# Three score windows and one turn window cut from one six-bank PSUM tile, in the attention of a hybrid transformer block

## Chip, cores and metric

The kernel runs on one core of a Trainium2 chip, in one launch. The metric is device time in microseconds (us). Several executions of a kernel are timed; one more is taken with the hardware profiler, and all rows shown here are from that one.

## The reference, cut to what matters

One layer: a conditioned RMSNorm of 512 latent tokens (and 256 context tokens) of width 2048, one input projection, then two branches. Branch A is attention with 12 query heads on 4 groups of keys and values, over 512 + 256 = 768 keys. Branch B is a Fourier mixing of 512 channels. Both are gated, projected, merged with sigmoid gates and projected once more, and a final RMSNorm follows. All in float32.

```python
q = _rope(_rmsnorm(_heads(p, OFF_Q, N_Q_HEADS), q_norm_g[l]), cos, sin) * q_scale
s = jnp.einsum('bqhgd,bkhd->bhgqk', qi, k, preferred_element_type=jnp.float32)
w = jax.nn.softmax(s, axis=-1).astype(v.dtype)
o = jnp.einsum('bhgqk,bkhd->bqhgd', w, v)
y_a = (attn * jax.nn.silu(z_a)) @ w_pa
y_b = (_fourier_mix(u_b) * jax.nn.silu(z_b)) @ w_pb
return (g_a * y_a + g_b * y_b) @ w_o
```

## The kernel before

Products in float32 are made of three matmuls (`mm3`, lines 294 to 298): each operand is split into a high and a low half (`split_from`, lines 161 to 163: ACT copies the high half, DVE subtracts it and so makes the low half), and high x high, high x low and low x high are added up in PSUM. The kernel is written in a framework that finds out itself which instruction must wait for which, orders each engine's instructions with a scheduler, and writes the waits into the program. So the order on an engine need not be that of the source.

The work has these stages:
- normalisation and the first columns of the input projection, and branch B's Fourier mixing (lines 408 to 658);
- eight groups of the input projection (lines 1028 to 1067), each with seven products of a fast matrix scheme (`Group.run`, line 734);
- the attention, a loop of 48 steps (lines 1185 to 1218), one for each head and 128 queries;
- the projection of branch A with the merge (lines 1278 to 1326);
- two output groups with the final norm (lines 1472 to 1489).

**PSUM** has eight banks of 512 float32 columns. From line 668 to the end one pool `psp` holds it. `pair` (line 695) gives a tile of two banks: the tag x has two buffers that take turns, and the tags y0 and y1 have one each, which alternate too.

A step of the attention takes these parts:
- `scores` (line 1115) takes the next x tile and writes 768 columns of it in six matmuls, 512 and 256 columns wide. DVE finds the negative maximum (line 1124), ACT the exponential with its sum (line 1126; a small second instruction reads the sum).
- `turn` (line 1138) transposes the probabilities of the step before, six transposes into the tile that holds the other of the y tags (`turned_y`, lines 1076 and 1140), and `split_from` makes their high and low halves, `pth` and `ptl`. `divide` takes the reciprocal of the sum and scales the gate.
- `values` (line 1149), once for two steps, multiplies the turned probabilities with the values: 18 matmuls of 256 columns and two transposes.
- `turn_queries` (line 1021) turns the queries of the next head, once for four steps.
- `filler` (line 1082) is work of branch B's projection, cut in 64 pieces of three matmuls, put between the parts of a step; `fill` asks for the next pieces. After every four pieces a copy (line 1102) takes the sum out.

`both` (line 1077) is one y tile for the whole attention: the first bank, `fill_acc`, is the fillings' accumulator, the second, `b1`, that of `values` and of the query turns. `get_keys` (line 1012) turns the keys of a group in an x tile; group 0's come before the attention, those of groups 1 to 3 in it.

In the last step the first two products of branch A's projection begin (`products`, line 1173; `first_sums`, line 1214). From there on `pair` serves the accumulators (line 1287), the turned merge (`turn_merged`, line 1235) and the output groups. In the very last product `Banks` (line 712) holds the sums as two x tiles, and `finish` (line 792) does the 24 matmuls of the first 128 tokens, calls `last` (line 1425), whose lines 1433 to 1437 read these sums, and then does the other 24.

Loads go over the queues of SP (weights, keys, values: `start_load`, line 183) and POOL (heads, line 1010).

Of the kernel before, what the change touches and what calls it, by code (L numbers as in the profile page):

```python
# [10 lines left out]
F32 = mybir.dt.float32  # L11
# [4 lines left out]
PSUM = bass.MemoryType.PSUM  # L16
DRAM = bass.MemoryType.DRAM

P = 128
# [8 lines left out]
NKEY = T + C  # L28
# [79 lines left out]
def block_kernel(ctx, tc, xT, ctx_rows, ctx_toks, x, c_row, w_ss, w_gate, vecs, qkg, rope, dft_c, dft_s,  # L108
# [4 lines left out]
    def region(name, side="left", **kw):  # L113
        st = ExitStack()
        return st, st.enter_context(tc.tile_pool(name=name, bufs=1, side=side, **kw))
# [22 lines left out]
    def uid(s):  # L138
        cnt[0] += 1
        return f"{s}{cnt[0]}"  # L140
# [20 lines left out]
    def split_from(src, hi, lo):  # L161
        nc.scalar.activation(hi, src, ACT.Copy)  # L162
        return nc.vector.tensor_tensor(lo, src, hi.bitcast(F32), op=ALU.subtract)  # L163
# [94 lines left out]
    def get(key):  # L258
        load_more()
        turn = [e for e in ahead if not e.aside]  # L260
        assert turn[0].key == key, (turn[0].key, key)
        for e in turn[: min(look[0], len(hl_pools))]:
            split_piece(e)
        load_more()
        e = turn[0]
        ahead.remove(e)
        free.extend(p[0::2] for p, _ in e.raws if p in retired)
        return e.raws[0][1] if e.kind == "raw" else e.out
# [15 lines left out]
    def take(shape, dt=F32, pool=None):  # L284
        p = next((p for p in free if p[0] is pool), free[0])
        free.remove(p)
        t = slot_tile(p, shape, dt)
        home[id(t)] = p, t
        return t

    def give(*ts):
        free.extend(home.pop(id(t))[0] for t in ts)

    def mm3(o, ah, al, bh, bl, start, stop, cont=False):

        nc.tensor.matmul(o, ah, bh, start=start, stop=False, skip_group_check=cont)  # L296
        nc.tensor.matmul(o, ah, bl, start=False, stop=False, skip_group_check=cont)  # L297
        nc.tensor.matmul(o, al, bh, start=False, stop=stop, skip_group_check=cont)  # L298
# [34 lines left out]
    def tiles(key):  # L333

        new = [take((1024,), F32R) for _ in range(2)]
        kept.setdefault(key, []).extend(new)
        return new
# [15 lines left out]
    flat = lambda v: v.rearrange("p t c -> p (t c)")  # L353
# [14 lines left out]
    for g in range(LAST + 1):  # L368
        for name in ONE_GROUP:
            if (g, name) == (LAST, "Q4"):  # L370
                stream_keys(0)
            if g == KV:
                f = CTX_FORMS.index(next(f for n, f, _, _ in PRODUCTS if n == name))
# [291 lines left out]
    evs, evp = region("evp", "right", reuse_waits="tile")  # L665
    new_ev = lambda: evp.tile([P, 2, 512], F32, tag="ev", bufs=4, name=uid("ev"))
    qzs, qzp = region("qzp", "right", reuse_waits="tile")
    psp = ctx.enter_context(tc.tile_pool(name="psp", bufs=1, space=PSUM, reuse_waits="tile"))
    last_y = [0]
    rows4 = lambda hi, lo: [(hi[:, j, :], lo[:, j, :]) for j in range(4)]  # L670

    def make_form(f, h):
# [20 lines left out]
        return rows4(hi, lo)  # L693

    def pair(tag, skip=0):
        if tag == "y":
            last_y[0] += 1 + skip
            return psp.tile([P, 2, 512], F32, tag=f"y{last_y[0] % 2}", bufs=1, name=uid(tag))
        return psp.tile([P, 2, 512], F32, tag=tag, bufs=2, name=uid(tag))
# [12 lines left out]
    class Banks:  # L712


        def __init__(self):
            self.b = [pair("x") for _ in range(2)]
# [4 lines left out]
    class Group:  # L721
# [12 lines left out]
        def run(self, name):  # L734
            form, which = next((f, c) for n, f, _, c in PRODUCTS if n == name)
            start = which not in self.acc
            if start:

                self.acc[which] = Banks() if self.last and which == "c" else pair(self.tags[which])
# [137 lines left out]
    class Context:  # L877
# [13 lines left out]
        def products(self, name, which, pc, w, start):  # L891
            a = self.acc[:, 1 if which == "b" else 0, :]
            for k in range(2):
                j = 2 * pc + k
                fh, fl = (f.parts[j // 4][:, j % 4 // 2, P * (j % 2) : P * (j % 2) + P] for f in self.f)
                mm3(a, fh, fl, w[0][:, k, :], w[1][:, k, :], start and pc == 0 and k == 0, pc == 3 and k == 1,
                    cont=not start)
# [23 lines left out]
        def values(self, b, v):  # L921
            nc.scalar.dma_start(by_group(v_d[:, :, 4 + b, :]), v.rearrange("p (g d) -> p g d", g=4))
# [60 lines left out]
    def load_row(half):  # L983
        row = crow[half] = take((1024,)) if half else rp.tile([P, 1024], F32, tag="raw1", bufs=1, name=uid("crow"))
        nc.gpsimd.dma_start(row, c_row[:, 1024 * half : 1024 * half + 1024].broadcast_to([P, 1024]))

    def silu_of_row(half):

        e, row = take((1024,)), crow[half]
        nc.scalar.activation(e, row, ACT.Tanh, scale=0.5)  # L990
        nc.vector.scalar_tensor_tensor(row, e, 1.0, row, op0=ALU.add, op1=ALU.mult)
        give(e)
# [15 lines left out]
    def load_head(h):  # L1008
        qz[h] = take((2, 4, HD))
        nc.gpsimd.dma_start(qz[h], qz_d[h])  # L1010

    def get_keys(g):
        raw = get(("K", g))
        tk = flat(pair("x"))
        for t in range(KT):
            nc.tensor.transpose(tk[:, t * P : (t + 1) * P], raw[:, t * P : (t + 1) * P], ident)
        keys = tiles(g)
        split_from(tk[:, :NKEY], *(w[:, :NKEY] for w in keys))
        kv[g] = tuple(keys) + get(("V", g))

    def turn_queries(h, tq):
        for t in range(4):
            nc.tensor.transpose(tq[:, t * P : (t + 1) * P], qz[h][:, 0, t, :], ident)
        qs[h] = take((2, T), F32R)
        split_from(tq, qs[h][:, 0, :], qs[h][:, 1, :])
# [47 lines left out]
    free += [(hm, f"s{(9 + i) % KK}") for i in range(KK)]  # L1073
    ats_, atp = region("atp", "right", reuse_waits="tile")

    turned_y = last_y[0] % 2
    both = pair("y")
    fill_acc, b1 = both[:, 0, :], lambda: both[:, 1, :]
    assert not any(p[0] is gvp or p[2] == "raw1" for e in ahead for p, _ in e.raws)
    ybs, S = {}, {}  # L1080

# [26 lines left out]
    def fill(n):  # L1108
        for _ in range(n):
            next(fl, None)  # L1110
# [4 lines left out]
    def scores(i):  # L1115
        h, t = divmod(i, 4)
        kh, kl = kv[h // GQ][:2]
        s = slice(t * P, (t + 1) * P)
        qh, ql = qs[h][:, 0, s], qs[h][:, 1, s]
        sc = flat(pair("x"))  # L1120
        for a, b in ((0, 512), (512, 768)):
            mm3(sc[:, a:b], qh, ql, kh[:, a:b], kl[:, a:b], True, True)
        mx = stats[:, 4 * (i % 4) : 4 * (i % 4) + 4]
        nc.vector.tensor_reduce(mx[:, 0:1], sc[:, :NKEY], axis=AX.X, op=ALU.max, negate=True)
        probs[i] = take((NKEY,))
        nc.scalar.activation(probs[i], sc[:, :NKEY], ACT.Exp, bias=mx[:, 0:1], accum_out=mx[:, 1:2])  # L1126
        if t == 3:
            give(qs.pop(h))

    def divide(i):  # L1130

        h, t = divmod(i, 4)
        z = qz[h][:, 1, t, :]
        r = stats[:, 4 * (i % 4) + 2 : 4 * (i % 4) + 3]
        nc.vector.reciprocal(r, stats[:, 4 * (i % 4) + 1 : 4 * (i % 4) + 2])
        nc.vector.tensor_scalar(z, z, r, None, op0=ALU.mult)

    def turn(i):
        p = probs.pop(i)
        tp = flat(psp.tile([P, 2, 512], F32, tag=f"y{turned_y}", bufs=1, name=uid("tp")))  # L1140
        for k in range(KT):
            nc.tensor.transpose(tp[:, k * P : (k + 1) * P], p[:, k * P : (k + 1) * P], ident)
        if i % 2 == 0:
            pts[i // 2] = [atp.tile([P, KT, 256], F32R, tag=n, bufs=2, name=uid(n)) for n in ("pth", "ptl")]
        c = slice((i % 2) * P, (i % 2) * P + P)
        split_from(tp[:, :NKEY].rearrange("p (k q) -> p k q", k=KT), *(w[:, :, c] for w in pts[i // 2]))
        give(p)
# [34 lines left out]
                        pc == 0 and k == 0, pc == BRANCH_A[-1] and k == 1)  # L1182
                yield pc, t

    filled = 0
    for i in range(NSTEP + 3):
        h, t = divmod(i, 4)
        if i < NSTEP:
            if t == 1 and h + 2 < NH:
                load_head(h + 2)  # L1190
            if i == 24:
                load_row(0)
            elif i == 28:
                silu_of_row(0)
            if i % 12 == 10 and i // 12 + 1 < NKV:
                get_keys(i // 12 + 1)
            scores(i)
        want = min(3 + 61 * (i + 1) // NSTEP, 64)
        if want > filled:
            fill(1)  # L1200
            filled += 1
        if i % 2 == 0 and i >= 4:
            values((i - 4) // 2)
        if 1 <= i <= NSTEP:
            turn(i - 1)
            divide(i - 1)
        if t == 1 and h + 1 < NH:
            turn_queries(h + 1, b1())
        if want > filled:
            fill(want - filled)  # L1210
            filled = want
        if i == NSTEP - 1:
            fill(1)
            first_sums = [pair("x") for _ in range(2)]
            first = products(CHUNKS[0], first_sums)
        if NSTEP > i - 2 >= NSTEP - 3:
            next(first)
            next(first)
# [12 lines left out]
    m = -1  # L1231
# [46 lines left out]
    for n, j in enumerate(CHUNKS):  # L1278
# [9 lines left out]
        for pc, t in products(j, accs) if n else first:  # L1288
# [4 lines left out]
            if pc > 3:  # L1293
                y = ybs[j, pc - 4]
# [274 lines left out]
```

## Time and profile before

| | us |
|---|---|
| median of 3 runs | 1335.85 |
| lowest and highest | 1332.83 and 1336.69 |
| the profiled execution | 1333.12 |
| its span, first to last instruction | 1331.3 |
| TensorE (PE) busy in it | 1298.5 |
| DVE, ACT and POOL busy | 977.9, 653.2 and 137.1 |
| the attention, first scores to last turn | 824.5 to 1027.3 |

A row of a group reads: line, engine, operation, what is written and read, shapes and count; then the busy time and the mean of one in nanoseconds; then the idle time of the engine just ahead of these instructions and who ended it. A row of a timeline reads: start, duration, engine, line, operation, and in brackets idle time ahead of it. A row of the waits reads: who waited for whom, us in total, how often, and the longest.

### The profile page before, as it was taken

How to read it: one execution, taken by the hardware profiler on the slowest of the kernel's cores; microseconds unless marked ns; L12 is line 12 of the kernel's file. 1: busy time of each engine (PE TensorE's matmuls, PEld its weight loads, DVE VectorE, ACT ScalarE, POOL GpSimd, SP SyncE). 2: the span in 40 equal slices, each digit the busy share in tenths (PEclk: the TensorE clock that was granted, in tenths of full speed). 3: DMA queues.
4: the chain of work that ended last, by engine and by line, in shares of the span. 5: the costliest groups of instructions: out<-in, count | busy, mean ns of one | idle time of the engine just before them, and what ended most of it. 6: DMA issues, size and time to landing. Idle time of an engine off the chain costs nothing. (4 is left out here: it accounts for less than half of the span.)

```text
span 1331.3 us, 17479 instructions
## 1 busy us (share of the span) xinstructions
PE 1298.5 (98%) x6594; PEld 1061.9 (80%) x6594; DVE 977.9 (73%) x1286; ACT 653.2 (49%) x1017; POOL 137.1 (10%) x186
## 2 busy tenths in 40 slices
PE   6999999999999999999999999999999999999996
PEld 3566888888888887888887888788888888887885
DVE  4655989887778867646477666677776789777677
ACT  5322655555555544544264455666665133364444
POOL 1110011210302011011021110000000100111210
PEclk9999999999999999999999999999999999999999
DMA  9996677887897999777669886122113899678983
GB/s 380 402 387 243 227 190 197 228 230 223 195 317 189 304 268 267 255 166 182 190 181 308 217 240 227 31 71 80 43 53 112 328 329 333 181 172 224 224 216 142
DMA packets 96085, 291.28 MB, mean 219 GB/s; under 512 B 8960, under 2 KB 32000, under 8 KB 91648
## 3 DMA queue, kind: packets, MB, share of 16 engines
q1 hardware_dynamic: 51600, 172.95, 37.1%
q0 software_dynamic: 21936, 94.39, 29.0%
q10 hardware_dynamic: 22464, 22.81, 5.1%
q8 instruction: 52, 0.85, 0.3%
q14 instruction: 33, 0.27, 0.1%
HBM read 263.37 MB, written 26.75 MB: 218 GB/s over the span
## 5 line engine op out<-in xcount | busy, mean ns | idle before, releaser
L162 ACT ACTIVATE whi<-wr 128x1024 fp32r<-128x1024 f32 (+1 forms) x130 | 136.6, 1052 | 189.8 <-PE y L298 90.0
L296 PE MATMUL y<-whi,s 128*128 128x512 f32 x548 | 216.4, 395 | 1.1 <-ACT s L768 1.1
L297 PE MATMUL y<-wlo,s 128*128 128x512 f32 x548 | 214.0, 390 | 0.7 <-DVE wlo L163 0.7
L296 PE MATMUL x<-whi,s 128*128 128x512 f32 x548 | 214.1, 391 | 0.2 <-ACT s L765 0.2
L297 PE MATMUL x<-wlo,s 128*128 128x512 f32 x548 | 213.5, 390 | 0.1
L298 PE MATMUL y<-whi,s 128*128 128x512 f32 x548 | 213.4, 390 | 0.0
L298 PE MATMUL x<-whi,s 128*128 128x512 f32 x548 | 213.3, 389 | 0.0
L163 DVE TENSOR_TENSOR wlo<-wr,whi 128x1024 fp32r<-128x1024 f32 (+1 forms) x130 | 157.0, 1211 | 57.6 <-ACT whi L162 57.4
L162 ACT ACTIVATE whi<-R 128x1024 fp32r<-128x1024 f32 x115 | 121.6, 1059 | 128.3 <-PE y L298 55.5
L163 DVE TENSOR_TENSOR wlo<-R,whi 128x1024 fp32r<-128x1024 f32 x115 | 139.7, 1220 | 48.9 <-ACT whi L162 48.9
L296 PEld LDWEIGHTS y<-whi,s 128*128 128x128 f32 x548 | 102.9, 188 | 24.9 <-DVE s L1166 2.3
L296 PEld LDWEIGHTS x<-whi,s 128*128 128x128 f32 x548 | 102.9, 188 | 21.8 <-ACT s L765 0.5
L297 PEld LDWEIGHTS x<-wlo,s 128*128 128x128 f32 x548 | 102.9, 188 | 21.7 <-DVE wlo L163 0.6
L298 PEld LDWEIGHTS y<-whi,s 128*128 128x128 f32 x548 | 102.9, 188 | 21.6
L298 PEld LDWEIGHTS x<-whi,s 128*128 128x128 f32 x548 | 102.9, 188 | 21.4
L297 PEld LDWEIGHTS y<-wlo,s 128*128 128x128 f32 x548 | 103.0, 188 | 20.4 <-DVE wlo L163 1.1
L296 PE MATMUL x<-s,s 128*128 128x512 f32 (+1 forms) x274 | 104.5, 381 | 4.2 <-ACT s L1126 3.1
L297 PE MATMUL x<-s,s 128*128 128x512 f32 (+1 forms) x284 | 106.5, 375 | 0.0
L298 PE MATMUL x<-s,s 128*128 128x512 f32 (+1 forms) x284 | 106.1, 374 | 0.0
L252 POOL DMA_DIRECT2D R<-in_w_g x64 | 55.2, 863 | 423.6 <-DVE wlo L163 263.2
L162 ACT ACTIVATE s<-wr 128x512 fp32r<-128x512 f32 (+2 forms) x92 | 60.4, 675 | 57.4 <-PE y L298 17.2
L163 DVE TENSOR_TENSOR s<-wr,s 128x512 fp32r<-128x512 f32 (+2 forms) x92 | 65.8, 743 | 23.3 <-ACT s L162 21.8
(275 smaller groups left out, 2249.0 us busy)
## 6 DMA issues: line engine op xcount, KB each, us to landing
wr<-in_w_g SPq DMA_DIRECT2D x128, 512.0 KB, 4.9
R<-in_w_g POOLq DMA_DIRECT2D x64, 512.0 KB, 6.7
wa<-in_w_ss POOLq DMA_DIRECT2D x28, 1024.0 KB, 9.1
R<-in_w_g SPq DMA_DIRECT2D x32, 512.0 KB, 5.1
wr<-in_w_pab SPq DMA_DIRECT2D x32, 512.0 KB, 5.1
wr<-in_w_gate SPq DMA_DIRECT2D x32, 512.0 KB, 5.5
wr<-in_w_o SPq DMA_DIRECT2D x24, 512.0 KB, 6.9
R<-in_w_o POOLq DMA_DIRECT2D x24, 512.0 KB, 7.4
```

The source lines that it names most:

```text
L162: nc.scalar.activation(hi, src, ACT.Copy)
L163: return nc.vector.tensor_tensor(lo, src, hi.bitcast(F32), op=ALU.subtract)
L252: nc.gpsimd.dma_start(chain[e.pc], e.nxt, accum_op=ALU.add)
L296: nc.tensor.matmul(o, ah, bh, start=start, stop=False, skip_group_check=cont)
L297: nc.tensor.matmul(o, ah, bl, start=False, stop=False, skip_group_check=cont)
L298: nc.tensor.matmul(o, al, bh, start=False, stop=stop, skip_group_check=cont)
```

## The change

Ahead of the attention the pool of the groups is closed and a new one opened with two tiles, `banks6` of six banks and `banks2` of two.
- `wide` cuts the 3072 columns of `banks6` into four windows of 768. Windows 0 to 2 serve scores and key turns in turn (`next_wide`), window 3 the turned probabilities. Window 0 ends and window 1 begins in the middle of bank 1, and window 2 ends and window 3 begins in the middle of bank 4.
- For window 1 the scores are written as 256 and 512 columns instead of 512 and 256, so that no matmul crosses a bank.
- `fill_acc` and `b1` are the two banks of `banks2`.
- After the attention `pair` gives slices: x takes banks 0 and 1 or 2 and 3 of `banks6`, y takes banks 4 and 5 of it or `banks2`.
- Two filling pieces are asked for ahead of the first step; the count of all stays 64.

```diff
-    psp = ctx.enter_context(tc.tile_pool(name="psp", bufs=1, space=PSUM, reuse_waits="tile"))
+    pgs, psp = region("psp", None, space=PSUM, reuse_waits="tile")
     last_y = [0]
+
+    banks = []
...
     def pair(tag, skip=0):
+        if banks:
+            last_y[tag == "x"] += 1
+            b = 2 * (last_y[tag == "x"] % 2) + (4 if tag == "y" else 0)
+            return banks[0][:, b : b + 2, :] if b < 6 else banks[1]
...
+    turn_wide = [0]
+
+    def next_wide():
+        turn_wide[0] += 1
+        return wide[turn_wide[0] % 3]
+
     def get_keys(g):
         raw = get(("K", g))
-        tk = flat(pair("x"))
+        tk = next_wide() if g else flat(pair("x"))
...
-    turned_y = last_y[0] % 2
-    both = pair("y")
-    fill_acc, b1 = both[:, 0, :], lambda: both[:, 1, :]
+
+    pgs.close()
+    psq = ctx.enter_context(tc.tile_pool(name="psq", bufs=1, space=PSUM, reuse_waits="tile"))
+    banks += [psq.tile([P, n, 512], F32, name=f"banks{n}") for n in (6, 2)]
+    last_y[:] = [0, 0]
+    wide = [flat(banks[0])[:, NKEY * i : NKEY * i + NKEY] for i in range(4)]
+    fill_acc, b1 = banks[1][:, 0, :], lambda: banks[1][:, 1, :]
...
-        sc = flat(pair("x"))
-        for a, b in ((0, 512), (512, 768)):
+        sc = next_wide()
+
+        m = 512 if sc is not wide[1] else 256
+        for a, b in ((0, m), (m, NKEY)):
             mm3(sc[:, a:b], qh, ql, kh[:, a:b], kl[:, a:b], True, True)
...
-        tp = flat(psp.tile([P, 2, 512], F32, tag=f"y{turned_y}", bufs=1, name=uid("tp")))
+        tp = wide[3]
...
-    filled = 0
+
+    fill(2)
+    filled = 2
...
-            first_sums = [pair("x") for _ in range(2)]
+            first_sums = [banks[0][:, 2 * b : 2 * b + 2, :] for b in range(2)]
```

## The prediction

> **What bounds the kernel now.** I read the page first (busy time by engine), then the three stretches before, in and after the attention, then the list of waits of TensorE (PE) inside the attention, then its timeline.
>
> ```profile
> PE 1298.5 (98%) x6594; PEld 1061.9 (80%) x6594; DVE 977.9 (73%) x1286; ACT 653.2 (49%) x1017; POOL 137.1 (10%) x186
> ```
> ```profile
> 824.50:1027.30 202.80, 197.12 (x1304) 173.37 (x1303) 146.87 (x253) 126.97 (x222) 5.28 (x10) 1.00 0.21 69
> ```
> ```profile
> PE x L296 <- ACT s L1126: 3.1, 5, 1.1
> PE x L296 <- ACT s L162: 1.1, 1, 1.1
> PE x L1016 <- ACT s L1126: 0.6, 1, 0.6
> PE y L296 <- ACT s L1102: 0.6, 1, 0.6
> PE tp L1142 <- DVE ptl L163: 0.3, 1, 0.3
> ```
>
> PE bounds it: busy 98% of the span, and 197.1 of the 202.8 us of the attention (columns of a stretch: length, then busy PE, PE weight load, DVE, ACT, POOL, then clock and DMA). That is 202.8 / 48 = 4.22 us for each of 48 steps. The waits are the whole prize: 5.7 us in total, of which 4.8 us are score matmuls or key turns that wait for a score buffer.
>
> **How waits are placed.** The fourth wait above tells more than its 0.6 us. The same wait by group of instructions:
>
> ```profile
> L296 PE MATMUL y<-pth,s 128*128 128x256 f32 x144 | 40.8, 283 | 0.6 <-ACT s L1102 0.6
> ```
>
> This matmul (`values`) writes the second bank of the tile that line 1077 takes; the copy of line 1102 reads the first bank of that tile. Nothing that it reads or overwrites is touched by the copy, and still it waits. So a write waits for every earlier read of its *tile*, whatever bank or columns were read. In the kernel before, two score tiles (x) and the tile for turned probabilities are separate tiles. In the changed one all four windows are slices of one tile of six banks. The written order of the changed program, with the waits that its instructions carry, says the same; two neighbouring steps read (line numbers of the changed kernel, window by first column):
>
> ```
> PE  L1160 turn into column 2304    waits for ACT L1144, the exp that reads column 1536 (newest scores)
> PE  L296  scores into column 0     wait for DVE L163, the low half read from column 2304
> PE  L1160 turn into column 2304    waits for ACT L1144, the exp that reads column 0 (newest scores)
> PE  L296  scores into column 768   wait for DVE L163, the low half read from column 2304
> ```
>
> Each pair of columns lies in different banks or buffers, except 1536 with 2304. So of the three score buffers only one is ever in flight: scores, maximum, exp, turn of the step before, high half, low half, and only then the next scores. Where PE had other steps to run ahead with, it now has one closed chain per step.
>
> **The chain, priced.** Means of the operations, then the hand-overs between engines in timelines.
>
> ```profile
> L1124 DVE TENSOR_REDUCE gain<-x 128x1 f32<-128x768 f32 x48 | 45.3, 950 | 3.6 <-PE x L298 3.4
> L163 DVE TENSOR_TENSOR ptl<-tp,pth 128x768 fp32r<-128x768 f32 x48 | 45.9, 955 | 17.3 <-ACT pth L162 16.9
> L1126 ACT ACTIVATE s<-x,gain 128x768 f32<-128x768 f32 x48 | 43.2, 901 | 22.5 <-DVE gain L1124 19.9 <-DVE gain L1135 1.7 <-PE y L298 0.9
> L162 ACT ACTIVATE pth<-tp 128x768 fp32r<-128x768 f32 x48 | 38.9, 811 | 18.7 <-PE tp L1142 18.3
> ```
> ```profile
> 828.28 0.39 PE L296 MATMUL x<-s,s 128*128 128x512 f32 x1
> 828.50 0.39 PE L297 MATMUL x<-s,s 128*128 128x512 f32 x1
> ...
> 829.19 0.28 PE L298 MATMUL x<-s,s 128*128 128x256 f32 x1
> ...
> 834.56 0.50 PE L296 MATMUL x<-s,s 128*128 128x512 f32 x1 [1.08 <-ACT s L162]
> 834.90 0.40 PE L297 MATMUL x<-s,s 128*128 128x512 f32 x1
> 835.62 0.87 PE L1142 MATMUL tp<-ident,s 128*128 128x128 f32 x6 [0.33 <-DVE ptl L163]
> ```
> ```profile
> 834.62 0.94 DVE L163 TENSOR_TENSOR ptl<-tp,pth 128x768 fp32r<-128x768 f32 x1
> ```
> ```profile
> 847.14 0.89 ACT L1126 ACTIVATE s<-x,gain 128x768 f32<-128x768 f32 x1
> ...
> 847.92 0.20 ACT L1126 ACTIVATION_READ_ACCUMULATOR s<-x,gain 128x1 f32 x1
> ...
> 848.17 0.50 PE L296 MATMUL x<-s,s 128*128 128x512 f32 x1 [0.57 <-ACT s L1126]
> ```
> ```profile
> 873.98 0.95 DVE L1124 TENSOR_REDUCE gain<-x 128x1 f32<-128x768 f32 x1
> ...
> 874.96 0.90 ACT L1126 ACTIVATE s<-x,gain 128x768 f32<-128x768 f32 x1 [1.01 <-DVE gain L1124]
> ...
> 876.57 0.82 PE L1142 MATMUL tp<-ident,s 128*128 128x128 f32 x6
> ...
> 877.42 0.81 ACT L162 ACTIVATE pth<-tp 128x768 fp32r<-128x768 f32 x1 [0.28 <-PE tp L1142]
> ...
> 878.26 0.96 DVE L163 TENSOR_TENSOR ptl<-tp,pth 128x768 fp32r<-128x768 f32 x1 [0.67 <-ACT pth L162]
> ```
>
> Six score matmuls run from 828.28 to 829.47, 1.19 us; after a wait the second starts 0.34 us after the first instead of 0.22, so 1.30. Maximum 0.95. Exp from its start to the end of its accumulator read, 847.14 to 848.12, 0.98. Six turns after a wait 0.87. High half 0.81, low half 0.955. Hand-overs: PE to ACT 0.03 (877.39 to 877.42), and I give PE to DVE the same; DVE to ACT 0.03 and ACT to DVE 0.03; ACT to PE 0.05 (848.12 to 848.17); DVE to PE 0.06 (835.56 to 835.62): 0.23. Sum 1.30 + 0.95 + 0.98 + 0.87 + 0.81 + 0.955 + 0.23 = **6.1 us** a step, against 4.22. 48 steps: 293.
>
> PE's other work is no bound: of 197.1 us, the chain's own matmuls take about 1.7 us a step, so 2.4 us of values, fillings and query turns are left, and the chain leaves PE two openings of 2.0 us (maximum, exp) and 1.9 us (both halves).
>
> Three key turns (groups 1 to 3) now use the windows too and stand in the same chain:
>
> ```profile
> L1016 PE MATMUL x<-ident,wr 128*128 128x128 f32 x24 | 3.5, 275 | 0.6 <-ACT s L1126 0.6
> L162 ACT ACTIVATE s<-x 128x768 fp32r<-128x768 f32 x3 | 2.4, 813 | 0.0
> L163 DVE TENSOR_TENSOR s<-x,s 128x768 fp32r<-128x768 f32 x3 | 2.9, 950 | 0.2 <-ACT s L162 0.2
> ```
>
> Each adds six turns like those above (0.87), 0.81, 0.95 and hand-overs: 2.8, together 8. The stage becomes 293 + 8 = 301 against 202.8: **+98**.
>
> Queueing inside the chain is not shown by the trace before. ACT is busy 127.0 us in the stage, of which 48 x (0.98 + 0.81) = 86 are the chain's: 41 of other work, splits and copies. DVE has 146.9 - 48 x 1.905 = 55, of which about 21 (reciprocal and scaling) run while PE turns. Nothing of it in the way gives 0; all of it gives 75. Both engines idle over half of each step in the new chain, so most of it fits; in the written order some 35 such rows (query turns, filling copies, weight splits) stand directly ahead of a chain row, at perhaps 0.3 us each. I take **+10**, near the low end.
>
> **After the attention** the accumulators x, and every other y, are slices of the same tile until the end, so an evacuation blocks the next product also where buffers alternate.
>
> ```profile
> PE y L296 <- ACT s L768: 1.1, 1, 1.1
> ```
> ```profile
> 1319.84 0.42 DVE L1433 TENSOR_TENSOR s<-x,s 128x256 f32<-128x256 f32 x1
> ```
> ```profile
> 1315.21 0.39 PE L296 MATMUL x<-whi,s 128*128 128x512 f32 x1
> ```
>
> One such wait costs 1.1 us today. The order holds about five more (copies of X and Y, one of the turned merge, one gate product): +6, between 0 and 8. The worst is the last: the second 24 matmuls of the final product started at 1315.21; now they wait for the second read of line 1433 of the first half, which ended at 1320.26: **+5**.
>
> **The other parts.** Two filling steps ahead of the scores are 6 matmuls, 0.22 us apart, that would run later anyway; they cover a new wait of the first scores for the last group's evacuation:
>
> ```profile
> L762 DVE TENSOR_TENSOR ev<-x,ev 128x1024 f32<-128x1024 f32 x1 | 1.2, 1224 | 0.4 <-PE x L298 0.4
> ```
>
> 1.22 plus hand-overs 0.1 against 1.3: nothing; without the cover +1.3. Splitting window 1's scores as 256 + 512 keeps the six matmuls. The loads of the filling keep their places in SP's queue; after the attention a few gate and projection loads swap, with 100 us more lead. POOL's head loads are unchanged.
>
> **Sum.** The profiled execution took 1333.1 us (span 1331.3): 1333.1 + 98 + 10 + 11 = 1452, and it lay 2.7 under the median of the three runs; so against that median **1455 us**, +9%.
>
> **Rivals.**
> *The change does what it says* (faster). Place: the scores' wait for a buffer, 4.8 us of the quoted waits; it decides if a score write waits only for reads of its own columns. 1335.85 - 5 = 1331. Against it stand the quoted wait of values on the copy of another bank, and the written order. The Trainium skill ("Perfetto Trace Analysis", Matmuls) says that independent matmul groups should rotate through banks so that evacuation overlaps the next group; by that rule this is the outcome. No run here shows it yet. Chance 0.03.
> *Waits go by bank.* Windows 0 and 1 share a bank, and window 2 and the turn window: one step in three waits for exp, one for the low half. 16 x 2.0 + 16 x 1.9 = 62 if PE had nothing to put there, 0 if its 2.4 us fit; nearer the low end, 1340. The same two pieces of evidence speak against it. Chance 0.03.
> *The clock falls.* PE would be busy 2 us in 3, in bursts.
>
> ```profile
> 45.00:50.00 5.00, 3.85 (x26) 2.35 (x27) 2.35 (x6) 1.34 (x2) 0.72 (x2) 1.00 1.02 419
> 1320.00:1331.00 11.00, 0.90 (x4) 0.40 (x3) 5.09 (x15) 4.46 (x13) 0.00 (x0) 0.73 0.88 324
> ```
>
> Where PE was busy 3.85 of 5 us the granted clock was 1.00, and it fell (0.73) only where PE was all but idle for 11 us. At half clock 2.2 us more per step, 48 x 2.2 = +105: 1560. The Trainium skill ("TensorE: Matmul & The Clock Gate", A second HAM failure mode) reports clocks that oscillate when PE idles briefly between groups cycling through PSUM; the first of these rows speaks against it here, with longer runs of work. Chance 0.03.
>
> **How the numbers follow.** Forecast 0.91; faster 0.03, the bank case 0.03 (two thirds of it over 0.3%, about what a measurement of this kernel can tell from no change), clock 0.03. Range: no queueing and half of the later waits, 1335.85 + 98 - 4 (shorter hand-overs) + 5 = 1435; 30 of queueing and 13 later gives 1477; rounded out, 1430 to 1485, and the rivals are left out of it.
>
> **What would show it.** Right: PE in the attention busy near 65%, its waits headed by L296 on DVE L163 and L1160 on ACT L1144 with some 40 of each, a step of 6.1 to 6.6 us, the clock at 1.00, and one wait of about 5 us before the last 24 matmuls. Wrong: score matmuls that start while the low half of the turn window is still being read.

## The result, and the profile after

The changed kernel takes 1510.7 us (median of 6 runs, 1503.3 to 1517.8); the kernel before took 1334.8 us beside it. The ratio is **1.133, 95% interval 1.130 to 1.135**: 176 us slower. I had forecast 1455 and 1430 to 1485. The sign and the main mechanism were right; the size was not. The profiled execution has a span of 1510.3 us against 1331.3, 179.0 more.

First the page: the line of the engine that bounds the kernel, and the granted clock in 40 slices, before and after.

```profile
PEclk9999999999999999999999999999999999999999
```
```profile
PE 1368.9 (91%) x6594; PEld 1097.9 (73%) x6594; DVE 985.8 (65%) x1286; ACT 657.0 (44%) x1017; POOL 137.4 (9%) x186
...
PEclk9999999999999999999999989778889999999999
```

PE has the same 6594 matmuls and yet 70 us more of busy time. That is the first sign that matmuls themselves took longer, and the last line says where: the clock, at 9 in every slice before, is down to 7 and 8 in six slices that lie in the attention. In stretches (length, busy PE, weight load, DVE, ACT, POOL, then clock and DMA), the attention from the first maximum to the last low half, before and then after, and what comes behind it after:

```profile
825.80:1029.10 203.30, 197.62 (x1305) 173.70 (x1304) 146.90 (x254) 126.72 (x222) 4.75 (x9) 1.00 0.22 72
```
```profile
827.60:1178.10 350.50, 256.69 (x1291) 204.19 (x1289) 151.69 (x252) 128.62 (x221) 4.77 (x9) 0.86 0.13 41
1178.10:1510.30 332.20, 299.82 (x1319) 243.26 (x1319) 237.68 (x258) 125.80 (x162) 32.01 (x44) 0.97 0.74 215
```

Behind the attention the kernel before needs 302.2 us. So 147.2 of the 179.0 us are lost in the attention, 30.0 behind it, and the rest ahead of it, where the attention begins 1.8 later. The waits of PE from the start of the attention through the first chunk of branch A's projection:

```profile
PE banks L296 <- DVE ptl L163: 47.1, 40, 1.9
PE banks L1160 <- ACT s L1144: 16.4, 17, 2.1
PE banks L296 <- ACT pth L162: 12.4, 14, 1.2
PE banks L296 <- DVE s L163: 6.7, 11, 1.7
PE banks L296 <- DVE s L1334: 4.0, 1, 4.0
```

The first row is the wait that the forecast rests on: in 40 steps the scores stand until the low half of the turn window has been read. The second was forecast with the same count and has 17. In 16 more steps the turns also start 0.05 us after exp has ended, but PE had only just finished other work, so no wait shows; in 14 steps other work of PE held the turns up by 0.2 to 1.6 us.

One step at the full clock, from three timelines (DVE, ACT, PE), shows the chain link by link:

```profile
837.60 0.96 DVE L1142 TENSOR_REDUCE gain<-banks 128x1 f32<-128x768 f32 x1 [1.46 <-PE banks L298]
...
841.39 0.96 DVE L163 TENSOR_TENSOR ptl<-banks,pth 128x768 fp32r<-128x768 f32 x1 [1.29 <-ACT pth L162]
843.76 0.96 DVE L1142 TENSOR_REDUCE gain<-banks 128x1 f32<-128x768 f32 x1 [1.41 <-PE banks L298]
```
```profile
838.60 0.90 ACT L1144 ACTIVATE s<-banks,gain 128x768 f32<-128x768 f32 x1
839.40 0.19 ACT L1144 ACTIVATION_READ_ACCUMULATOR s<-banks,gain 128x1 f32 x1
840.55 0.81 ACT L162 ACTIVATE pth<-banks 128x768 fp32r<-128x768 f32 x1 [0.96 <-PE banks L1160]
```
```profile
839.64 0.87 PE L1160 MATMUL banks<-ident,s 128*128 128x128 f32 x6
841.41 0.38 PE L296 MATMUL banks<-pth,s 128*128 128x256 f32 x1 [0.90 <-ACT pth L162]
842.41 0.39 PE L296 MATMUL banks<-s,s 128*128 128x256 f32 x1 [0.61 <-DVE ptl L163]
...
843.34 0.39 PE L298 MATMUL banks<-s,s 128*128 128x512 f32 x1
```

Maximum 837.60 to 838.56, exp to 839.59, turns to 840.51, high half to 841.36, low half to 842.35, scores to 843.73, next maximum at 843.76: 6.16 us, where the forecast had 6.1. But 350.5 us for 48 steps are 7.3 each. Counted from maximum to maximum, 13 ordinary steps lie wholly at the full clock: they take 6.15 to 6.51 us, 6.32 in the mean. Two more at the full clock have key turns in them and take 9.0 and 9.4, so key turns cost about the 2.8 that I had given them. The others, but for a short first one, have a stretch in them like this:

```profile
948.40 0.50 PE L296 MATMUL banks<-s,s 128*128 128x512 f32 x1 [1.84 <-DVE ptl L163]
...
949.56 0.40 PE L296 MATMUL banks<-whi,s 128*128 128x512 f32 x1
949.79 0.59 PE L297 MATMUL banks<-wlo,s 128*128 128x512 f32 x1
950.18 0.63 PE L298 MATMUL banks<-whi,s 128*128 128x512 f32 x1
950.60 0.63 PE L296 MATMUL banks<-whi,s 128*128 128x512 f32 x1
```

A matmul of 512 columns follows the one before it after 0.23 us, and in the middle of this stretch that becomes 0.39 and then 0.42. Behind the first of these rows nothing was waited for; PE itself went at half its speed, and the clock granted from 949.84 on is 0.50.

### The profile page after: what moved, and what is told of

The parts are those of the page before. It is cut to its first block, busy times and chain, and to the rows that moved or that the text cites. A ratio compares the mean times of both kernels' runs of the same rounds, so it can differ in the third digit from the quotient of the medians.

```text
span 1510.3 us, 17476 instructions
## 1 busy us (share of the span) xinstructions
PE 1368.9 (91%) x6594; PEld 1097.9 (73%) x6594; DVE 985.8 (65%) x1286; ACT 657.0 (44%) x1017; POOL 137.4 (9%) x186
## 3 DMA queue, kind: packets, MB, share of 16 engines
q0 software_dynamic: 21936, 94.39, 25.7%
## 4 chain that ended last, share of the span: by engine, by line
PE 74%; DVE 10%; ACT 6%; DMA 5%; issue 4%; POOL 0%; ACTq 0%; SPq 0%; DVEq 0%; POOLq 0%
PE banks L296 9%; PE banks L298 8%; PE banks L297 8%; PE x L297 6%; PE x L296 6%; PE x L298 6%; PE y L297 6%; PE y L298 6%; PE y L296 6%; DVE ptl L163 3%; PE banks L1160 2%; ACT pth L162 2%; DVE wlo L163 2%; PE pd L484 2%; PE pb L297 1%
## 5 line engine op out<-in xcount | busy, mean ns | idle before, releaser
L296 PE MATMUL banks<-whi,s 128*128 128x512 f32 x428 | 177.8, 415 | 33.1 <-DVE s L1334 5.1
L297 PE MATMUL banks<-wlo,s 128*128 128x512 f32 x428 | 173.7, 406 | 0.0
L298 PE MATMUL banks<-whi,s 128*128 128x512 f32 x428 | 173.6, 406 | 0.0
L297 PE MATMUL x<-wlo,s 128*128 128x512 f32 x352 | 137.1, 389 | 0.7 <-DVE wlo L163 0.7
L296 PE MATMUL x<-whi,s 128*128 128x512 f32 x352 | 137.1, 390 | 0.0
L298 PE MATMUL x<-whi,s 128*128 128x512 f32 x352 | 137.0, 389 | 0.0
L296 PEld LDWEIGHTS banks<-whi,s 128*128 128x128 f32 x428 | 84.2, 197 | 61.2 <-ACT whi L162 8.6
L297 PE MATMUL y<-wlo,s 128*128 128x512 f32 x316 | 123.1, 389 | 0.8 <-DVE wlo L163 0.8
L296 PE MATMUL y<-whi,s 128*128 128x512 f32 x316 | 123.0, 389 | 0.0
L298 PE MATMUL y<-whi,s 128*128 128x512 f32 x316 | 122.8, 389 | 0.0
L296 PE MATMUL banks<-s,s 128*128 128x512 f32 (+1 forms) x148 | 62.7, 424 | 48.9 <-DVE ptl L163 44.6
L298 PEld LDWEIGHTS banks<-whi,s 128*128 128x128 f32 x428 | 84.2, 197 | 18.7
L297 PEld LDWEIGHTS banks<-wlo,s 128*128 128x128 f32 x428 | 84.3, 197 | 15.8
L163 DVE TENSOR_TENSOR ptl<-banks,pth 128x768 fp32r<-128x768 f32 x48 | 46.0, 958 | 66.4 <-ACT pth L162 66.4
```

## Experiments

The theory after the result: (a) waits go by tile and close the chain, worth the +98 and +10 of the forecast; (b) the clock falls in the openings of the chain, some 30 us; (c) waits behind the attention cost more than I gave them. The rivals: the shared banks do it; the reopened pool or the early fillings do it; there is no clock effect, and queueing is larger than forecast.

**Four tiles in the reopened pool.** All of the change but the cutting of one tile: pool reopened, fillings first, and two score tiles, a turn tile and one for the accumulators.

```diff
-            b = 2 * (last_y[tag == "x"] % 2) + (4 if tag == "y" else 0)
-            return banks[0][:, b : b + 2, :] if b < 6 else banks[1]
+            return banks[last_y[tag == "x"] % 2 + (2 if tag == "y" else 0)]
...
-    banks += [psq.tile([P, n, 512], F32, name=f"banks{n}") for n in (6, 2)]
+    banks += [psq.tile([P, 2, 512], F32, name=f"banks{n}") for n in range(4)]
...
-    wide = [flat(banks[0])[:, NKEY * i : NKEY * i + NKEY] for i in range(4)]
+    wide = [flat(banks[i])[:, :NKEY] for i in range(3)]
```

> The changed kernel with four tiles of two banks in the reopened pool instead of six banks and two: two score windows and the turn window each in a tile of its own, the pool closed and opened at the same place, two fillings first. Theory T (waits go by whole tile, and the windows in one tile close the chain): nothing is left of the loss, 1328 to 1340 us, the attention near 203 us, clock 1.00. Rival R (closing and reopening the pool, or the fillings put first, delays the work): part of the 176 us stays, over 1350 us.

Measured: 1332.8 us, ratio 0.9997 (0.9987 to 1.0007). The attention takes 200.9 us. Reopening the pool and asking for two pieces first cost nothing; the whole loss lies in the cutting.

**No shared bank.** The tile of six banks stays, but its windows begin at columns 0, 1024 and 2048, so no two meet in a bank; two serve scores.

```diff
-        return wide[turn_wide[0] % 3]
+        return wide[turn_wide[0] % 2]
...
-    wide = [flat(banks[0])[:, NKEY * i : NKEY * i + NKEY] for i in range(4)]
+    wide = [flat(banks[0])[:, 1024 * i : 1024 * i + NKEY] for i in range(3)]
...
-        tp = wide[3]
+        tp = wide[2]
```

> The changed kernel with its six-bank tile, but two score windows and the turn window at columns 0, 1024 and 2048, so that no bank holds parts of two windows. Theory T: the tile is still one, so every write still waits for every earlier read: 1490 to 1525 us, the attention near 350 us. Rival B (windows that share a bank collide or wait there): no bank is shared, so 1330 to 1345 us.

Measured: 1509.0 us, ratio 1.131 (1.127 to 1.135), the attention 350.8 us, and the same wait heads its list:

```profile
PE banks L296 <- DVE ptl L163: 47.5, 40, 1.9
```

Shared banks play no part; the waits go by tile. Both kernels open this pool with `reuse_waits="tile"`, and no run changed that, so whether this setting is what makes the tile the unit stays open. The run also shows that the third score window, which was the point of the cutting, changes nothing.

**The turn window in a tile of its own.** Two score windows stay in one tile of four banks; the pool opens again, with separate tiles, after the first chunk.

```diff
+    banks += [psq.tile([P, n, 512], F32, name=f"banks{n}_{i}") for i, n in enumerate((4, 2, 2))]
...
+    wide = [flat(banks[0])[:, 1024 * i : 1024 * i + NKEY] for i in range(2)] + [flat(banks[2])[:, :NKEY]]
```

> As the run before, with the turn window taken out into a tile of two banks; two score windows stay together in one tile of four banks. Theory T: the chain is cut to scores, maximum, exp, next scores, 1.3 + 0.95 + 0.98 + 0.1 = 3.4 us, shorter than the 4.2 us of matmuls in a step: PE is hardly held, clock near 1.00, 1335 to 1360 us. If any two windows in one tile cost as much as three (the tile itself is slow, not the chain): over 1420 us.

Measured: 1362.5 us, ratio 1.021 (1.019 to 1.023), a little over the range that I gave. The attention and the wait that heads its list:

```profile
828.10:1051.90 223.80, 202.19 (x1299) 172.72 (x1298) 148.56 (x252) 125.59 (x221) 4.77 (x9) 1.00 0.19 64
```
```profile
PE banks L296 <- ACT s L1142: 13.4, 16, 1.7
PE banks L1026 <- ACT s L1142: 3.2, 2, 1.7
```

Scores still wait for the exp of the other window, but only 16 times: PE has turns, values and fillings to run meanwhile. 20 us are lost instead of 147, and the clock stays at 1.00. What closes the long chain is that the *turns* share a tile with the scores.

**Separate tiles after the first chunk.** The attention as changed; from the second chunk of branch A's projection on, tiles as before.

```diff
+    pqs, psq = region("psq", None, space=PSUM, reuse_waits="tile")
...
+        if n == 1:
+            pqs.close()
+            banks.clear()
+            psp = ctx.enter_context(tc.tile_pool(name="psr", bufs=1, space=PSUM, reuse_waits="tile"))
+            last_y[:] = [0, 0]
```

> The changed kernel, whose pool is closed after the first chunk of the branch A projection and replaced by the separate tiles of the kernel before; the attention is untouched. Theory T: of the 30 us lost behind the attention some 20 to 25 come back, the first wait of 4 us stays: 1485 to 1495 us, and the attention stays near 350 us. Rival (the loss behind the attention comes from loads that arrive late or from a clock that stays low): 1505 to 1515 us.

Measured: 1487.9 us, ratio 1.116 (1.112 to 1.119). The part behind the attention goes from 332.2 to 308.1 us, so 24 of its 30.0 are due to slices from the second chunk on. The attention takes 347.3 here.

**The tail alone.** The opposite: four tiles in the attention, and the tiles of six and two banks after the first chunk.

```diff
+    banks += [psq.tile([P, 2, 512], F32, name=f"banks{n}") for n in range(4)]
...
+        if n == 1:
+            pqs.close()
+            psr = ctx.enter_context(tc.tile_pool(name="psr", bufs=1, space=PSUM, reuse_waits="tile"))
+            banks[:] = [psr.tile([P, n2, 512], F32, name=f"after{n2}") for n2 in (6, 2)]
```

> The attention with four tiles of two banks, as fast as before; after the first chunk of branch A the pool is opened again with one tile of six banks and one of two, as the changed kernel has them there. It is the opposite of the run that had separate tiles after the first chunk and gave back 23 us. If the waits after the attention cost by themselves and don't come from a clock that the attention left low, the part after the attention is some 18 to 25 us longer than before: 1350 to 1359 us. If that part is long only because the slow attention comes ahead of it (its clock, or loads that come at another time), it stays within 5 us of the kernel before: under 1340. My forecast had priced these waits at 11: 1344.

Measured: 1359.4 us, ratio 1.019 (1.017 to 1.021), at the upper edge of what I gave for the first case. The attention takes 200.9 us, the part behind it 328.7:

```profile
1027.30:1356.00 328.70, 297.54 (x1312) 241.67 (x1310) 237.65 (x257) 125.78 (x162) 31.93 (x44) 0.98 0.74 219
```

That is 25.7 us over the 303.0 of the run with four tiles, with a fast attention ahead of it. So the loss does not come from the attention, and it is more than twice what I had priced. It is not all waiting: 19 us of it are idle time of PE, and in the rest PE is busy longer (297.5 us against 290.9), with some 9 us more at half clock than in the run with four tiles.

**Matmuls in the opening.** This pair measures the clock. In the first kernel the tile has five banks (two score windows and the turn window), two banks serve the accumulators, and one bank is spare; separate tiles come back after the first chunk. The second adds six matmuls behind each turn, which write the spare bank and whose result nobody reads: work that the reference does not need.

```diff
+        return wide[turn_wide[0] % 2]
...
+    banks += [psq.tile([P, n, 512], F32, name=f"banks{n}") for n in (5, 2, 1)]
...
+    wide = [flat(banks[0])[:, NKEY * i : NKEY * i + NKEY] for i in range(3)]
```
```diff
+    def keep_busy(n, ins):
...
+        with tc.issue_after(ins.ins):
+            for _ in range(n):
+                nc.tensor.matmul(banks[2][:, 0, :], kh[:, :P], kh[:, :512], start=True, stop=True)
...
+        keep_busy(6, last)
```

> Separate tiles again after the first chunk, as in the run with that edit alone; in the attention the shared tile has five banks, with two score windows and the turn window, and one bank is left unused. Theory T: only one score window is ever in flight, so two windows give what three gave: the same time as with three, 1480 to 1500 us, clock 0.83 to 0.90 in the attention. If the third window did buy something, this is slower by 10 us or more.

> The same with six matmuls more behind each turn, into the spare bank, which nobody reads: 288 matmuls of 512 columns, 65 us of PE time at full clock, put where PE waits for the two halves. Theory C (the granted clock falls because PE idles in each step): the clock is 0.95 or more in the attention, the steps come to 6.2 to 6.6 us and the attention to 305 to 325 us, so 1445 to 1465 us, faster with more work. Rival (the clock falls for another reason, or the chain is longer than worked out): no faster, 1480 to 1530 us.

Measured: 1482.8 us without (ratio 1.114, 1.108 to 1.120) and **1454.6 us with** (1.090, 1.087 to 1.092). The attention without, then with them:

```profile
827.30:1174.20 346.90, 251.91 (x1291) 200.96 (x1290) 151.71 (x252) 128.39 (x221) 4.75 (x9) 0.87 0.13 42
```
```profile
830.90:1146.70 315.80, 277.01 (x1579) 223.92 (x1577) 153.38 (x252) 129.65 (x221) 4.75 (x9) 0.99 0.14 46
```

288 more matmuls, and 31 us less in the attention: the clock goes from 0.87 to 0.99. What stays, 315.8 us, is the closed chain at nearly the full clock. The 13 ordinary steps at the full clock of the changed kernel say about the same without any added matmul: 48 x 6.32 and 8 or 9 for the key turns are 312.

**Half the dose.** Three matmuls behind each turn instead of six.

```diff
-        keep_busy(6, last)
+        keep_busy(3, last)
```

> Two windows, a turn window and a spare bank in one tile of five banks, with three idle matmuls after each turn instead of six (144 more than in the kernel without them, 144 fewer than in that with six). The chain of hand-overs is the same in all three, about 6.6 us a step at the full clock. If the granted clock falls by the share of a step that PE idles, three matmuls (0.7 us of each step) give a time between the two, 1455 to 1480 us, with the mean clock in the attention between 0.87 and 0.99: near the low end if a small filling is enough, near 1475 to 1483 if only an opening shorter than some bound counts. If the six matmuls helped by something else than the clock, the clock and the time don't go together.

Measured: 1457.6 us, ratio 1.092 (1.090 to 1.095). The attention:

```profile
829.90:1150.30 320.40, 253.94 (x1435) 200.51 (x1433) 151.49 (x252) 128.98 (x221) 4.75 (x9) 0.97 0.14 45
```

Half of the filling gives 26.5 of the 31 us, and clock and time go together over the three kernels. That is not proportional to the filling: it looks like a threshold, which the next section looks for in the trace.

**The filling's accumulator in its own tile.** If a wait goes by tile, the kernel before has one to lose: values wait for the copy of the fillings' bank. Four tiles as in the first experiment, but `fill_acc` and `b1` in a one-bank tile each, and four pairs again after the first chunk.

```diff
+    banks += [psq.tile([P, 2 if n < 3 else 1, 512], F32, name=f"banks{n}") for n in range(5)]
...
+    fill_acc, b1 = banks[3][:, 0, :], lambda: banks[4][:, 0, :]
...
+        if n == 1:
+            pqs.close()
+            psr = ctx.enter_context(tc.tile_pool(name="psr", bufs=1, space=PSUM, reuse_waits="tile"))
+            banks[:] = [psr.tile([P, 2, 512], F32, name=f"after{q}") for q in range(4)]
```

> The four tiles of two banks (as in the run with four tiles), but the fillings' accumulator and that of values stand in a one-bank tile each, and after the first chunk of branch A the pool is opened again with four tiles of two banks. Waits go by tile: the wait of values on the copy of the fillings' accumulator (0.6 us in the profile before, one wait of 0.6) must be gone from the list of waits; nothing else changes. Time 1328 to 1336 us, at most 1 us under the kernel before, which 0.3% cannot tell. If waits went by bank the wait would not have been there to remove, and if it stays, the tile is not what decides it.

Measured: **1326.1 us, ratio 0.9936 (0.9919 to 0.9953)**, 7.5 us under the kernel before. I had expected at most 1: a miss, on the good side. The attention takes 194.3 us against 200.9 with four tiles, and PE idles 0.3 us in it against 4.7. PE's waits from the attention to the end, with four tiles and then with the split:

```profile
PE banks L296 <- ACT s L1143: 3.0, 4, 1.0
PE banks L296 <- ACT s L773: 1.1, 1, 1.1
PE banks L296 <- ACT s L1117: 0.6, 1, 0.6
PE banks L1027 <- ACT s L1143: 0.5, 1, 0.5
```
```profile
PE after L296 <- ACT s L773: 1.1, 1, 1.1
PE after L297 <- DVE wlo L163: 0.6, 1, 0.6
PE after L296 <- ACT s L770: 0.2, 1, 0.2
PE banks L296 <- ACT s L1143: 0.2, 1, 0.2
```

The wait for the copy (L1117) is gone as expected, and with it nearly all waits of scores for exp (L1143), which the edit doesn't touch. The order of PE's instructions is another one from the first steps on, perhaps since the scheduler no longer has to keep fillings, query turns and values in step through one tile; that reason is not shown. Whether the shorter waits or the new order alone gives the 6.6 us was not separated. This version beats both kernels: it gets what the change was after, fewer waits of scores for a buffer, by dividing a tile and not by joining several.

## Why the prediction was wrong in size

**Waits go by tile: right.** The 40 waits of scores for the low half are there; the run without shared banks takes out the bank rival, and the run with four tiles leaves nothing else to blame. The rival "does what it says" falls with it. The Trainium skill ("Perfetto Trace Analysis", Matmuls) says that groups should rotate through banks so that evacuation overlaps the next group's matmuls. From windows of one tile no such overlap came here: three rotating windows took 1510.7 us, and two that share no bank 1509.0.

**The chain of 6.1 us: right.** Each link of the step shown is within 0.03 us of its term. **Queueing, +10: about right.** The closed chain at the full clock took 315.8 - 203.3 = 112.5 more, against 98 + 10.

**The clock: wrong, and this is the step that failed.** I had it as a rival that is all or nothing, half clock in all 48 steps for +105, gave it 0.03 and left it out of the range. It fell in part of the steps: some 99 of the 350.5 us are at half clock. The pair of runs prices it at 31 us where 89 us at half clock became 3. The argument against it was a mean: PE busy in 3.85 of 5 us at full clock. With the 31 and the 3.6 of the sum below, the clock in the attention cost some 35 us. Without them the time would have been about 1476, inside my range; without only the 19 us that the part behind the attention cost over my 11, about 1492.

The trace of the changed kernel shows what goes with the clock. The stretches at half clock last 3.41 us or a multiple of it, on one grid. Twelve cells of that grid in a row:

```profile
925.95:929.37 3.42, 1.91 (x11) 1.31 (x10) 0.96 (x1) 1.40 (x2) 0.00 (x0) 1.00 0.18 73
929.37:932.78 3.41, 3.40 (x26) 3.04 (x26) 1.12 (x2) 0.99 (x2) 0.00 (x0) 1.00 0.00 0
932.78:936.19 3.41, 1.56 (x10) 1.25 (x10) 1.58 (x3) 1.07 (x2) 0.00 (x0) 1.00 0.01 2
936.19:939.60 3.41, 3.41 (x13) 2.61 (x12) 1.37 (x3) 1.33 (x3) 0.00 (x0) 0.50 0.00 0
939.60:943.02 3.42, 2.60 (x15) 1.90 (x14) 1.68 (x3) 1.07 (x2) 0.00 (x0) 1.00 0.00 0
943.02:946.43 3.41, 3.40 (x27) 2.99 (x25) 1.41 (x3) 0.99 (x2) 0.00 (x0) 1.00 0.03 5
946.43:949.84 3.41, 1.57 (x10) 1.26 (x9) 1.75 (x3) 1.71 (x3) 0.00 (x0) 1.00 0.00 0
949.84:953.25 3.41, 2.73 (x7) 1.74 (x6) 1.10 (x2) 1.13 (x2) 0.00 (x0) 0.50 0.00 0
953.25:956.67 3.42, 2.52 (x10) 1.72 (x9) 0.55 (x3) 1.17 (x3) 0.00 (x0) 0.50 0.00 0
956.67:960.08 3.41, 3.00 (x9) 2.41 (x10) 1.03 (x2) 0.17 (x1) 0.00 (x0) 0.50 0.00 0
960.08:963.49 3.41, 3.41 (x18) 3.41 (x17) 1.23 (x3) 1.66 (x3) 0.00 (x0) 0.50 0.00 0
963.49:966.91 3.42, 1.58 (x13) 1.34 (x12) 2.19 (x3) 1.07 (x2) 0.00 (x0) 1.00 0.18 19
```

Read PE's busy time (second number) and then the clock (third from the end) of the *next* row. Behind 1.91, 3.40 and 2.60 us of work the clock stays at 1.00; behind 1.56 and 1.57 it is 0.50. At 0.50 it stays behind 2.73, 2.52 and 3.00, and it comes back behind a full cell. Over the whole attention, 20 cells at full clock are followed by one at half: PE was busy 0.37 to 0.56 of these, 19 of them at most 0.48. 52 are followed by one at full clock, and PE was busy at least 0.51 of 50 of those, 0.47 and 0.495 of the other two. (The ends of matmuls in a trace are modelled, so a share close to the edge is not exact.) So what counts here is not PE's mean (256.7 of 350.5 us, well above half) but each cell, and the two openings of 2 us in a step of 6.2 leave some cells less than half full. That explains the dose too: in the attention with no matmuls added, with three and with six, 20, 4 and 1 cells are followed by a fall, and 26, 5 and 1 cells are at half clock.

The Trainium skill ("TensorE: Matmul & The Clock Gate", Part 1) states a free-running window of 3413 ns and two clocks, half and full; the trace agrees with both. The rule of thumb of the Trainium skill (the same page, "HAM oscillation — how this bites in real kernels"), to leave PE no idle gap over some 3.4 us, is too mild here: no wait of the attention is over 2.1 us, and the clock fell 20 times.

**After the attention, +11: too small.** It is 25.7 by the run of the tail alone. In the changed kernel PE waits there 14 times, 22.4 us in all:

```profile
PE banks L296 <- DVE s L1334: 5.1, 2, 4.0
PE banks L296 <- DVE s L768: 4.3, 3, 1.5
PE banks L296 <- ACT s L771: 3.3, 2, 2.1
PE banks L296 <- DVE s L1390: 2.8, 1, 2.8
...
PE banks L296 <- DVE s L1453: 1.5, 1, 1.5
```

I had counted on about five more waits at 1.1 each and one of 5 at the end. There are 14 and not some seven, and the two longest end with reads by DVE. Their 22.4 us are not the whole 30.0 either: PE is also busy 9.5 us longer there than before (299.8 us against 290.3), at a mean clock of 0.97 against 0.99. I had given the clock nothing behind the attention. Ahead of the longest, PE was done with the first chunk at 1245.2; DVE had weights to split and scale until 1246.7, and then read both sums of the chunk:

```profile
1246.70 2.35 DVE L1334 TENSOR_TENSOR s<-banks,s 128x1024 f32<-128x1024 f32 x2
```

At 1249.2 PE went on, after 4.0 us. The one wait that I called the worst, ahead of the last 24 matmuls, is the last row: 1.5 instead of 5.

**The sum.** 112.5 chain + 31.1 clock + 3.6 more in the attention + 30.0 behind it + 1.8 ahead of it = 179.0. The 3.6 separates the changed kernel from the kernel with two windows and a spare bank; the changed one has some 10 us more at half clock, which at 31 us for 85 would be 3.7 (an estimate). Of the 30.0 the tail alone explains 25.7. The remaining 4 were not separated: that run has a fast attention ahead, but also separate tiles in the first chunk.

## What to carry to other kernels

Find out which unit the framework's waits go by before cutting buffers out of one allocation: here a wait on one bank's reader by a writer of another bank, 0.6 us long in the profile before, gave away both the loss of 176 us and a gain of 7.5. When a change opens holes in the busiest engine, don't weigh the clock by a mean or as all or nothing: lay cells of the length that the clock's changes show in a trace (3.41 us here) over the new step, and count those in which the engine is less than half busy. A range should hold a partial form of every rival that shares its cause with the forecast.

## What was unexpected of the hardware

A kernel got 28 us faster by 288 matmuls that compute nothing (1482.8 to 1454.6 us), since they kept TensorE's granted clock at 0.99 instead of 0.87. And the clock is slow to come back: at half clock, cells in which PE was busy 2.52 to 3.00 of 3.41 us did not bring it back (19 returns in the attention all came behind cells at least 0.90 busy), so a cell that falls short can cost up to four in a row, 949.84 to 963.49 us. The edge is not sharp by this measure: in the kernel with two windows and a spare bank one return came behind a cell busy 0.79, and in the changed kernel the clock stayed at half behind one busy 0.88.
